# Splitting the rotated queries and keys of a decoder block over 128 rows, with the halves placed by DMA, and one step of the wide rsqrt on ScalarE

## The chip, the cores and the metric

The kernel runs on one core of a Trainium2 chip. Its engines work side by side, each on its own instruction stream: TensorE (matrix products; PE in the profile, its weight loads PEld), VectorE (DVE), ScalarE (ACT), GpSimd (POOL) and SyncE (SP). SP does nothing here but start DMAs; POOL starts those that add into their destination. All DMAs are carried out by the core's 16 DMA engines.

The metric is the time of one execution on the device in microseconds (us), lower is better. "Profiled execution" is the one execution that was recorded; its span is the time from its first to its last instruction.

## What is computed

The block has a causal pooling mixer and a causal differential attention side by side, then cross attention to a memory, then a squared-ReLU MLP, each with RMS norms. The change touches the attention's queries and keys, and the RMS norms. Cut to that (4 heads, each with 2 maps of width 64; sequence 512; model width 1024):

```python
h = rms_norm(x, g_mix)                        # x * rsqrt(mean(x*x) + 1e-6) * g
u, q, k, v, gate_logits = split(h @ w_in)
q = apply_rope(q.reshape(B, S, 4, 2, 64))     # t1*cos - t2*sin, t2*cos + t1*sin
k = apply_rope(k.reshape(B, S, 4, 2, 64))
s = einsum('bqhcd,bkhcd->bhcqk', q, k) * 64 ** -0.5
p = softmax(where(kpos <= qpos, s, -1e30))
a = p[:, :, 0] - lam * p[:, :, 1]
o = rms_norm(a @ v, g_subln) * (1 - lam_init)
```

Inputs and output are float32. The products run in a faster float32 form (`F32R` in the code), and to keep the accuracy each operand is given as a sum of two parts: a high part, the operand cast to `F32R`, and a low part, the operand minus its high part. A full product is then three matmuls: high by high, high by low, low by high.

## The kernel before

Everything is laid out with features on the 128 partitions ("rows") and the 512 positions along the free dimension. The order of TensorE's instructions is the program's own order, written out by hand: `PLAN` gives the order of the projection tiles, `k0 q0 q1 k1 q2 q3 g4 k2 g5 g6 k3 g7 u0 u1 u2 u3 g0 g1 g2 g3`, after the value projection. Each tile is eight steps of three matmuls (`tile_mm`, lines 316 to 322, `mm3`, lines 116 to 119). After each step a counter goes up by one (`tick`), and work that is due at that count is put in (`after`, `run_due`). So the scores of head h for the query block i are put in at count 36 + 6 (4 h + i) (`START`, `SPACE`, lines 593 to 595); the first, of head 0 and block 0, four steps into tile q2. The orders of the other engines and of the DMA queues are not written out: a planner arranges them when the program is built, from a model of the durations, and from then on they are fixed. Each engine then works through its list in order and waits, by semaphores, for what each instruction needs.

A projection tile of q or k (`qk_proj`, lines 443 to 462) holds one head: 128 rows, two maps of 64 (`c` is 0 or 1), with columns of the weights so arranged that the two halves of a rotation lie in neighbouring rows. VectorE multiplies the product by the table of sines into `b` and by that of cosines into `a` (lines 447 and 448). Two DMAs on POOL's queue add the neighbouring rows of `b` into `a` (line 450), and `a` is then the rotated tile. What the scores need is `s`, with 128 rows and a column block for each map c: for map 0 the high part in rows 0 to 63 and the low part in rows 64 to 127, for map 1 the other way round. One matmul over 128 rows then sums high times high and low times low (line 472), and a second one with `z`, which is the k tile with its row halves exchanged, adds high times low and low times high (line 473). The halves of `s` are written by four instructions of 64 rows each: ScalarE casts (lines 453 and 455), VectorE subtracts (lines 454 and 456), the latter reading one half of the rows and writing the other. For a k tile two DMAs on SP's queue copy `s` with its halves exchanged into `z` (lines 460 and 461), each 64 rows of 1024 values.

`tmp()` has 10 buffers of 128 x 512 in this part of the program; `a` and `b` are two of them. `s` and `z` are from a set of 6 buffers: k0, z0, q0, q1, k1 and z1 fill it, and q2, q3 and k2 can be written only after the last scores of head 0 have been read, z2, k3 and z3 only after those of head 1. The scores' products go to three PSUM banks (`sc`), and each is given back when VectorE has read it (line 476).

`split` (lines 122 to 124) makes a high and a low part of one width: a cast on ScalarE and a subtraction on VectorE. `rsqrt` (lines 242 to 251) makes rsqrt(sum * scale + eps): VectorE writes the mean plus epsilon `v` (line 244), ScalarE makes the logarithm from the same sum (line 245), an exponential (246) and a square (247), and VectorE corrects the result with `v` by one Newton step (248 and 251). It is called with a width of 512 by the first norm and by each of the four attention heads (`finish`, lines 512 to 518), with a width of 256 by the memory's norm, and with widths of 4 and 8 by the rest. `M` is 256.

Weights of the next tiles come in by loads on SP's queue (line 162), 512 KB each into three buffers `wraw`, and are split by ScalarE (line 123) and VectorE (line 124).

Of the kernel before, what the change touches and what calls it, by code (L numbers as in the profile page):

```python
# [12 lines left out]
F32R = mybir.dt.float32r  # L13
AF = mybir.ActivationFunctionType
ALU = mybir.AluOpType
# [7 lines left out]
M = 256  # L23
# [4 lines left out]
EPS = 1e-6  # L28
# [26 lines left out]
def block_kernel(ctx: ExitStack, tc: tile.TileContext, x0g, xT, memT, wv, wm, wst, wcq, wdn, wckv, wpool, vecs, csts, idn, gfin, out):  # L55
    nc = tc.nc
    ctx.enter_context(tc.manual_schedule(engines={mybir.EngineType.PE}))
    pool = ctx.enter_context(tc.tile_pool(name="sb", bufs=1))
    first, early = ExitStack(), ExitStack()
# [24 lines left out]
    def sb(tag, shape, bufs, dt=F32):  # L84
        if tag in MID_TAGS and not late:
            return mid["pool"].tile(shape, dt, tag=tag, name=nm(tag), bufs=bufs)
        if tag in STAGE_TAGS and not late:
            return stage.tile(shape, dt, tag=tag, name=nm(tag), bufs=bufs)
        p = apool if tag in EARLY_TAGS else late["pool"] if tag in LATE_TAGS else pool
        return p.tile(shape, dt, tag=tag, name=nm(tag), bufs=bufs)  # L90

    def tmp(dt=F32):
        return sb("tmp", [P, T], 3 if late else 10, dt)
# [4 lines left out]
    def pair(tag, bufs):  # L98
        return sb(tag, [P, 2, T], bufs, F32R)
# [4 lines left out]
    def acc():  # L104
        return ps("acc", 2)

    def f(ap):
        return ap.bitcast(F32)

    V = nc.vector  # L110
# [3 lines left out]
    S = nc.scalar  # L114
# [7 lines left out]
    def split(hi, lo, src, eng=V):  # L122
        S.copy(hi, src)  # L123
        eng.tensor_tensor(lo, src, f(hi), op=ALU.subtract)  # L124
# [16 lines left out]
    eps = home[:, 560:561]  # L141
# [99 lines left out]

    def rsqrt(dst, ssum, scale, v, l, by=None):

        V.tensor_scalar(v, ssum, scale, EPS, op0=ALU.mult, op1=ALU.add)
        S.activation(l, ssum, AF.Ln, bias=eps, scale=scale)
        S.activation(dst, l, AF.Exp, scale=-0.5)
        S.activation(l, dst, AF.Square)
        V.scalar_tensor_tensor(l, l, -0.5, v, op0=ALU.mult, op1=ALU.mult)
        if by is not None:
            by(dst)  # L250
        V.scalar_tensor_tensor(dst, l, 1.5, dst, op0=ALU.add, op1=ALU.mult)
# [11 lines left out]
    def rstd_full(sp, scratch, w=T):  # L263
        o = ps("tr", 2)[:, :w]
        bcast_sum(o, *sp)
        r = sb("rstd", [P, w], 1) if w == T else sb("mrstd", [P, w], 1)[:, :w]
        rsqrt(r, o, 1.0 / D, scratch, tmp()[:, :w])
        return r

    def rstd_rows(sp, n):  # L270
        hi, lo = sp
        o = ps("tr", 2)
        for i in range(n):
            c = slice(i * P, (i + 1) * P)
            nc.tensor.matmul(o[:, 2 * i:2 * i + 2], hi[:, c], ones[:, :2], start=True, stop=False)
            nc.tensor.matmul(o[:, 2 * i:2 * i + 2], lo[:, c], ones[:, :2], start=False, stop=True)
        r = sb("rrow", [P, 16], 2)[:, :2 * n]
        rsqrt(r, o[:, :2 * n], 1.0 / D, sb("rscr", [P, 8], 4)[:, :2 * n], sb("rscr", [P, 8], 4)[:, :2 * n])
        return r
# [36 lines left out]
    def tile_mm(o, w, rhs, ks=range(KC), first=True, last=True):  # L316
        ks = list(ks)
        for n, k in enumerate(ks):
            c = slice(k * P, (k + 1) * P)
            mm3(o, w[0][:, c], w[1][:, c], rhs[k][0], rhs[k][1],  # L320
                first and n == 0, last and n == len(ks) - 1)
            tick()
# [33 lines left out]
    def W(*key):  # L356
        return weights(where[key])
# [85 lines left out]
    def qk_proj(which, h):  # L443
        o = acc()
        tile_mm(o, W(which, h), xg)
        a, b = tmp(), tmp()
        V.tensor_tensor(b, o, sin_r, op=ALU.mult)
        V.tensor_tensor(a, o, cos_r, op=ALU.mult)
        for j in range(2):
            nc.gpsimd.dma_start(a[j::2, :], b[1 - j::2, :], accum_op=ALU.add)  # L450
        s = pair("s", 6)
        top, bot = slice(0, 64), slice(64, 128)
        S.copy(s[top, 0, :], a[top, :])
        V.tensor_tensor(s[bot, 0, :], a[top, :], f(s[top, 0, :]), op=ALU.subtract)
        S.copy(s[bot, 1, :], a[bot, :])
        V.tensor_tensor(s[top, 1, :], a[bot, :], f(s[bot, 1, :]), op=ALU.subtract)
        st[which, h] = s
        if which == "k":
            z = pair("s", 6)
            nc.sync.dma_start(f(z[top, :, :]), f(s[bot, :, :]))  # L460
            nc.sync.dma_start(f(z[bot, :, :]), f(s[top, :, :]))
            st["z", h] = z


# [35 lines left out]
    def attend(h):  # L500
        at = st["at", h]
        o = ps("av", 1)
        e = slice(h * P, (h + 1) * P)
        for b in range(NT):
            vh, vl = st["v"][b]
            mm3(o[:, b * P:], vh[:, e], vl[:, e], at[0][:, b, b * P:], at[1][:, b, b * P:],
                b == 0, b == NT - 1)
        sq = tmp()
        S.activation(sq, o, AF.Square)
        sp = split_sq(sq, T)  # L510

        def finish():
            s = ps("tr", 2)
            bcast_sum(s, *sp)
            y = tmp()
            rsqrt(y, s, 1.0 / P, sq, tmp(),
                  lambda r: V.scalar_tensor_tensor(r, o, st["gsub"], r, op0=ALU.mult, op1=ALU.mult))
            merge(4 + h, y)

        after(FINISH, finish)  # L520
# [68 lines left out]

    v_proj()  # L590
    tiles = {"q": lambda m: qk_proj("q", m), "k": lambda m: qk_proj("k", m), "g": gate_proj, "u": u_proj}
    for n, (kind, m) in enumerate(plan):
        if n == 2:
# [348 lines left out]
    rows = {}  # L942
# [298 lines left out]
```

## Time and profile before

| | us |
|---|---|
| three runs | 695.05, 696.56, 696.99 |
| median | 696.56 |
| profiled execution, its own time | 696.08 |
| its span | 694.3 |
| granted TensorE clock over the span | 0.996 of full speed |

The page of the profile gives each engine's busy time and then cuts the span into 40 slices of 17.4 us:

```
## 2 busy tenths in 40 slices
PE   9999999899999999999999999999999999999995
DVE  7688899886577998897488699967997779868996
ACT  7445888659655875565376967457844776367853
PEclk9999999999999999999999999999999999999999
```

Each digit is a busy share in tenths, and 9 means 90% or more. The q and k tiles, the scores and the pooling lie between 27 us and about 165 us, that is in slices 2 to 10. PE is busy nearly throughout; DVE and ACT have slices of eight or nine tenths there. Three more views are used below: the waits of an engine (who waited, for whom, how long), stretches of the span with the busy time of each engine, the granted clock and the share of the DMA engines that was busy, and the timeline, with each instruction's start and duration.

### The profile page before, as it was taken

The numbers are of one execution on the slowest core, as the hardware profiler recorded it, in microseconds if no ns is written. First come the engines' busy times: TensorE is split into PE (matmuls) and PEld (weight loads), VectorE is DVE, ScalarE is ACT, GpSimd is POOL, SyncE is SP. The second block draws the span as 40 slices with busy tenths as digits, with TensorE's granted clock in tenths as the row PEclk, the third lists the DMA queues.
The fourth block names the chain that finished last, engine by engine and source line by source line (L and its number), as shares of the span: only waits on it lengthen the run. The fifth ranks groups of instructions, "written<-read, shape, count | busy, mean of one in ns | idle before, by whom it ended". The sixth has DMA issues, their size and how long they took to land.

```text
span 694.3 us, 10735 instructions
## 1 busy us (share of the span) xinstructions
PE 682.1 (98%) x4024; PEld 603.2 (87%) x4024; DVE 562.0 (81%) x867; ACT 449.3 (65%) x726; POOL 82.3 (12%) x87
## 2 busy tenths in 40 slices
PE   9999999899999999999999999999999999999995
PEld 6888887788889979998889998899888998899884
DVE  7688899886577998897488699967997779868996
ACT  7445888659655875565376967457844776367853
POOL 0022101544210000000100011100100001100200
PEclk9999999999999999999999999999999999999999
DMA  8565325115484454430782179966688578967713
GB/s 311 173 162 157 92 82 155 67 35 209 152 244 147 156 182 121 109 106 31 209 245 92 64 202 237 257 213 183 156 246 241 153 180 211 268 182 184 167 46 121
DMA packets 34275, 113.66 MB, mean 164 GB/s; under 512 B 3984, under 2 KB 4624, under 8 KB 34224
## 3 DMA queue, kind: packets, MB, share of 16 engines
q1 hardware_dynamic: 26416, 87.42, 36.0%
q0 software_dynamic: 7664, 25.30, 20.5%
q8 instruction: 31, 0.51, 0.3%
q10 hardware_dynamic: 144, 0.26, 0.1%
q14 instruction: 20, 0.16, 0.1%
HBM read 106.68 MB, written 2.10 MB: 157 GB/s over the span
## 4 chain that ended last, share of the span: by engine, by line
PE 57%; DVE 1%; ACT 0%; DVEq 0%; issue 0%
PE sc L117 9%; PE sc L119 9%; PE sc L118 9%; PE acc L117 8%; PE acc L119 8%; PE acc L118 8%; PE tr L117 2%; PE tr L119 2%; PE tr L118 2%; PE tr L801 1%; PE tr L950 0%; PE acc L950 0%; ACT tmp L787 0%; PE av L119 0%; PE av L117 0%; PE av L118 0%
## 5 line engine op out<-in xcount | busy, mean ns | idle before, releaser
L123 ACT CAST whi<-wraw 128x1024 fp32r<-128x1024 f32 (+1 forms) x80 | 82.5, 1032 | 47.7 <-PE acc L118 16.7
L124 DVE TENSOR_TENSOR wlo<-wraw,whi 128x1024 fp32r<-128x1024 f32 (+1 forms) x80 | 97.4, 1219 | 14.5 <-ACT whi L123 14.1
L123 ACT CAST whi<-mraw 128x1024 fp32r<-128x1024 f32 x58 | 60.9, 1050 | 51.8 <-PE sc L118 14.5
L124 DVE TENSOR_TENSOR wlo<-mraw,whi 128x1024 fp32r<-128x1024 f32 x58 | 70.6, 1222 | 23.1 <-ACT whi L123 22.9
L117 PE MATMUL acc<-xg,whi 128*128 128x512 f32 x200 | 80.2, 401 | 0.0
L119 PE MATMUL acc<-xg,wlo 128*128 128x512 f32 x200 | 78.2, 391 | 0.0
L118 PE MATMUL acc<-xg,whi 128*128 128x512 f32 x200 | 78.0, 390 | 0.0
L124 DVE TENSOR_TENSOR mhl<-mraw,mhl 128x1024 fp32r<-128x1024 f32 x32 | 39.0, 1221 | 18.7 <-ACT mhl L123 18.5
L123 ACT CAST mhl<-mraw 128x1024 fp32r<-128x1024 f32 x32 | 33.7, 1052 | 30.6 <-PE sc L118 10.5
L119 PEld LDWEIGHTS acc<-xg,wlo 128*128 128x128 f32 x200 | 37.5, 188 | 8.2
L117 PEld LDWEIGHTS acc<-xg,whi 128*128 128x128 f32 x200 | 37.7, 189 | 7.2
L118 PEld LDWEIGHTS acc<-xg,whi 128*128 128x128 f32 x200 | 37.7, 189 | 7.0
L117 PE MATMUL sc<-mix,whi 128*128 128x256 f32 (+1 forms) x120 | 36.9, 307 | 0.0
L119 PE MATMUL sc<-mix,wlo 128*128 128x256 f32 (+1 forms) x120 | 36.2, 302 | 0.0
L118 PE MATMUL sc<-mix,whi 128*128 128x256 f32 (+1 forms) x120 | 36.1, 301 | 0.0
L123 ACT CAST xg<-raws 128x1024 fp32r<-128x1024 f32 x28 | 29.3, 1050 | 9.2 <-PE acc L118 4.7
L124 DVE TENSOR_TENSOR xg<-raws,xg 128x1024 fp32r<-128x1024 f32 x28 | 34.0, 1218 | 0.7 <-ACT xg L123 0.5
L184 POOL DMA_DIRECT2D mraw<-wdn x16 | 13.8, 864 | 171.1 <-DMA mraw<-wdn 79.0
L117 PE MATMUL acc<-mix,whi 128*128 128x256 f32 (+1 forms) x104 | 33.8, 325 | 0.0
L119 PE MATMUL acc<-mix,wlo 128*128 128x256 f32 (+1 forms) x104 | 33.6, 323 | 0.0
L118 PE MATMUL acc<-mix,whi 128*128 128x256 f32 (+1 forms) x104 | 33.4, 321 | 0.0
L184 POOL DMA_DIRECT2D mraw<-wst x16 | 13.8, 864 | 154.7 <-DMA mraw<-wst 95.8
(382 smaller groups left out, 2212.2 us busy)
## 6 DMA issues: line engine op xcount, KB each, us to landing
wraw<-wm SPq DMA_DIRECT2D x36, 512.0 KB, 3.3
mraw<-wst SPq DMA_DIRECT2D x24, 512.0 KB, 5.2
mraw<-wdn SPq DMA_DIRECT2D x24, 512.0 KB, 4.2
mraw<-wdn POOLq DMA_DIRECT2D x24, 512.0 KB, 7.3
wraw<-wckv SPq DMA_DIRECT2D x16, 512.0 KB, 3.7
mraw<-wst POOLq DMA_DIRECT2D x16, 512.0 KB, 7.2
wraw<-wst SPq DMA_DIRECT2D x16, 512.0 KB, 6.3
wraw<-wdn SPq DMA_DIRECT2D x16, 512.0 KB, 5.9
```

Source lines behind the costliest of these rows:

```text
L117: nc.tensor.matmul(o, lh, rh, start=start, stop=False, skip_group_check=free)
L118: nc.tensor.matmul(o, lh, rl, start=False, stop=False, skip_group_check=free)
L119: nc.tensor.matmul(o, ll, rh, start=False, stop=stop, skip_group_check=free)
L123: S.copy(hi, src)
L124: eng.tensor_tensor(lo, src, f(hi), op=ALU.subtract)
L184: nc.gpsimd.dma_start(r, part(key, then), accum_op=ALU.add)
L801: nc.tensor.transpose(tr[:, (2 * c + b) * P:(2 * c + b + 1) * P], e[:, b * M + c * P:b * M + (c + 1) * P], ident)
```

## The change

For a tile of q or k, the high and the low part are now made for all 128 rows at once by `split`, in `hi` (a further `tmp` buffer) and `lo` (the memory of `b`, whose sum has been added by then). `place` then brings their halves to `s` by four DMAs on SP's queue, each of 64 rows by 512 values, and for a k tile to `z` by four more, straight from `hi` and `lo` instead of from `s`. In `rsqrt`, where the width is 256 or more, ScalarE writes the mean plus epsilon, as an activation with a scale and a bias; the narrow ones stay on VectorE.

```diff
     def rsqrt(dst, ssum, scale, v, l, by=None):
 
-        V.tensor_scalar(v, ssum, scale, EPS, op0=ALU.mult, op1=ALU.add)
+        if v.shape[1] < M:
+            V.tensor_scalar(v, ssum, scale, EPS, op0=ALU.mult, op1=ALU.add)
+        else:
+            S.activation(v, ssum, AF.Identity, bias=eps, scale=scale)
         S.activation(l, ssum, AF.Ln, bias=eps, scale=scale)
...
         s = pair("s", 6)
         top, bot = slice(0, 64), slice(64, 128)
-        S.copy(s[top, 0, :], a[top, :])
-        V.tensor_tensor(s[bot, 0, :], a[top, :], f(s[top, 0, :]), op=ALU.subtract)
-        S.copy(s[bot, 1, :], a[bot, :])
-        V.tensor_tensor(s[top, 1, :], a[bot, :], f(s[bot, 1, :]), op=ALU.subtract)
+        hi, lo = tmp(F32R), b.bitcast(F32R)
+        split(hi, lo, a)
+
+        def place(to, first, second):
+            for c, rows in enumerate((top, bot)):
+                nc.sync.dma_start(f(to[top, c, :]), f((first, second)[c][rows, :]))
+                nc.sync.dma_start(f(to[bot, c, :]), f((second, first)[c][rows, :]))
+
+        place(s, hi, lo)
         st[which, h] = s
         if which == "k":
             z = pair("s", 6)
-            nc.sync.dma_start(f(z[top, :, :]), f(s[bot, :, :]))
-            nc.sync.dma_start(f(z[bot, :, :]), f(s[top, :, :]))
+            place(z, lo, hi)
             st["z", h] = z
```

## The prediction

> **What bounds the kernel now.** I read the page's busy times first, then what TensorE (PE) waits for, then stretches around each wait, then the timeline where the changed lines run.
>
> ```profile
> PE 682.1 (98%) x4024; PEld 603.2 (87%) x4024; DVE 562.0 (81%) x867; ACT 449.3 (65%) x726; POOL 82.3 (12%) x87
> PE sc L472 <- DVE small L476: 2.2, 1, 2.2
> PE av L118 <- DVE at L124: 0.9, 1, 0.9
> 106.81 0.50 PE L118 MATMUL av<-at,vr 128*128 128x512 f32 x1 [0.86 <-DVE at L124]
> 131.32 0.44 PE L472 MATMUL sc<-s,s 128*128 128x384 f32 x1 [2.25 <-DVE small L476]
> ```
>
> PE is busy 682.1 of 694.3 us, and its matmuls are the same in both kernels. So VectorE or ScalarE work saved is worth nothing in itself; it pays only where PE waits for it. In the attention part there are two such waits, both for VectorE (DVE): 0.86 us at 106 us and 2.25 us at 129 us. What a wait costs beyond itself shows in the stretches behind the second (columns: stretch, length, busy time of PE, PEld, DVE, ACT and POOL with instruction counts, granted clock, DMA share, GB/s):
>
> ```profile
> 130.00:132.00 2.00, 0.68 (x3) 0.65 (x4) 2.00 (x7) 1.64 (x4) 1.83 (x2) 0.98 0.00 0
> 132.00:134.00 2.00, 2.00 (x7) 1.76 (x6) 1.97 (x9) 1.10 (x4) 1.92 (x2) 0.50 0.25 66
> 134.00:136.00 2.00, 2.00 (x11) 1.87 (x10) 0.63 (x2) 0.80 (x4) 1.58 (x2) 0.66 0.52 205
> 106.00:108.00 2.00, 1.19 (x6) 1.10 (x7) 1.94 (x5) 1.95 (x4) 0.00 (x0) 1.00 0.71 262
> ```
>
> The granted clock falls to 0.50 and 0.66 of full speed for 2 us each. At half speed half the time is lost, so this loses 2 x 0.50 + 2 x 0.34 = 1.7 us more. Behind the 0.86 us wait the clock stays at 1.00. I therefore price a wait of over 2 us with a drop of 1.7 us, a shorter one without. So 0.9 + 2.25 + 1.7 = 4.8 us is all that the change could win here.
>
> [...]
>
> **What is removed.** Per tile, of eight:
>
> ```profile
> L453 ACT CAST s<-tmp x8: 602/621/622, 42.9 to 105.7; 64x512 fp32r<-64x512 f32 x8
> L456 DVE TENSOR_TENSOR s<-tmp,s x8: 687/687/687, 44.3 to 108.7; 64x512 fp32r<-64x512 f32 x8
> 102.83 0.62 ACT L123 CAST mix<-tmp 128x512 fp32r<-128x512 f32 x1 [1.17 <-DVE tmp L542]
> 104.87 0.69 DVE L124 TENSOR_TENSOR mix<-tmp,mix 128x512 fp32r<-128x512 f32 x1
> L244 DVE TENSOR_SCALAR tmp<-tr x4: 681/684/692, 92.8 to 163.8; 128x512 f32<-128x512 f32 x4
> L245 ACT ACTIVATE tmp<-tr,vx x6: 475/680/692, 30.5 to 206.8; 128x512 f32<-128x512 f32 x5, 128x256 f32<-128x256 f32 x1
> ```
>
> A cast takes 0.62 us and a subtraction 0.69 us, over 64 rows or 128. So one of each per tile goes: 8 x 0.62 = 5.0 us of ScalarE and 8 x 0.69 = 5.5 us of VectorE. The wide rsqrts move 0.68 us each for the first norm and four heads and about 0.42 us for the memory's (an estimate: the width of 256 is 0.48 us on line 245), 3.8 us in all, to ScalarE at about the same price. Their chain gets no longer: line 245 reads the same PSUM sum, and `v` is needed only three activations later. ScalarE is then about level, VectorE 9.3 us lighter.
>
> How much reaches PE is a smaller question, since VectorE catches up in between:
>
> ```profile
> 97.86 0.69 DVE L248 SCALAR_TENSOR_TENSOR tmp<-tmp,tmp 128x512 f32<-128x512 f32 x1 [0.30 <-ACT tmp L247]
> 113.50 0.69 DVE L476 CUSTOM_DVE_ANT_0 tmp<-sc,cst 128x512 f32<-128x512 f32 x1 [0.66 <-PE sc L473]
> 115.86 0.68 DVE L244 TENSOR_SCALAR tmp<-tr 128x512 f32<-128x512 f32 x1
> ```
>
> At 113.5 us VectorE waits for PE, so nothing saved before that shortens the wait at 129. Behind it only one removed instruction lies on VectorE, the 0.68 us at 115.86. At 97.86 it waits for ScalarE, which gets no lighter, and between there and the wait at 106 nothing is removed. Bounds of the gain: 0 and 4.8 us (the planner orders both engines anew and may clear both waits). I take 1.0 us: 0.68 at the second wait, whose drop stays, and about a third of the first.
>
> **What is added.** SP's queue gets four DMAs for each q tile and eight for each k tile in place of two, 48 for 8. Bytes go from 512 KB to 1024 KB per k tile, and from none to 512 KB per q tile. Above all, a q tile, which was finished by VectorE, is now finished by a DMA. That matters where PE reads soon after. The first scores (head 0, block 0) are that place:
>
> ```profile
> 44.35 0.52 SPq L460 DMA_DIRECT2D s<-s  x1
> 45.02 0.49 SPq L461 DMA_DIRECT2D s<-s  x1
> 47.48 6.89 SPq L162 DMA_DIRECT2D wraw<-wm  x2
> 49.49 0.62 ACT L453 CAST s<-tmp 64x512 fp32r<-64x512 f32 x1 [3.65 <-DMA tmp<-tmp]
> 50.14 0.69 DVE L454 TENSOR_TENSOR s<-tmp,s 64x512 fp32r<-64x512 f32 x1 [2.70 <-ACT s L453]
> 50.86 0.69 DVE L456 TENSOR_TENSOR s<-tmp,s 64x512 fp32r<-64x512 f32 x1
> 52.97 0.22 PE L472 MATMUL sc<-s,s 128*128 128x128 f32 x1
> 53.14 0.28 PE L472 MATMUL sc<-s,s 128*128 128x128 f32 x1
> ```
>
> q0's rotated tile lands at 49.4 us, its `s` is complete at 51.55, PE reads it at 52.97 (map 0) and 53.14 (map 1): 1.4 us to spare. After the change the low part is ready at 50.83 instead, the third and fourth DMAs, those of map 1, are issued behind it at half a microsecond each, the last at about 51.8. How long until it lands?
>
> ```profile
> out<-vr SPq DMA_DIRECT2D x2, 128.0 KB, 2.2
> DMA to landing us min/median/max: 2.9/4.4/5.2
> DMA to landing us min/median/max: 5.3/5.3/5.4
> 44.00:46.00 2.00, 2.00 (x11) 1.65 (x10) 1.94 (x4) 1.25 (x2) 0.27 (x1) 1.00 1.00 265
> 46.00:48.00 2.00, 2.00 (x11) 1.65 (x10) 1.45 (x2) 0.00 (x0) 1.14 (x2) 1.00 1.00 270
> 48.00:50.00 2.00, 2.00 (x10) 1.68 (x9) 0.00 (x0) 0.51 (x1) 0.55 (x1) 1.00 1.12 230
> 50.00:52.00 2.00, 2.00 (x10) 1.66 (x9) 1.79 (x3) 1.78 (x3) 0.00 (x0) 1.00 0.89 231
> 52.00:54.00 2.00, 2.00 (x13) 1.71 (x12) 2.00 (x3) 0.00 (x0) 0.59 (x2) 1.00 0.23 54
> ```
>
> The first row is the shortest 128 KB transfer of the list of DMA issues; the second is line 461 over the whole run, the third line 460 before 66 us (256 KB each). From below: 51.8 + 2.2 = 54.0, a wait of 0.9 us. With what such copies needed at that hour, 5.2 us: 57.0, a wait of 3.9. From above, by the work queued: the DMA engines are full from 44 to 52 us and busy 0.23 of the next two, and 512 KB more of k0 and 512 KB of q0 stand before the last landing; 1 MB at 265 GB/s is 4.0 us behind 52.5, then about a microsecond to land, 57.5 to 58, and k1's adding DMAs, which start then, share the engines: 59, a wait of 6. I take 3.9, from the row of the same place, and, being over 2 us, the clock drop of 1.7: 5.6 us.
>
> [...]
>
> The DMAs wait on SP for the cast and the subtraction. Behind k0's eight (from 43.5, its cast's end, to about 47.6 us) stands the weight load that now starts at 47.48: 0.1 us later. Behind q0's four stands the next one, which starts at 54 anyway (the row covers both): nothing. ScalarE, which waits for these loads to cast them, has the PE wait as cover. Without it the loads would land some 4 us late, and PE would stop at the next tile.
>
> Later tiles have more room. One place is tight:
>
> ```profile
> 59.41 0.62 ACT L453 CAST s<-tmp 64x512 fp32r<-64x512 f32 x1
> 72.30 0.22 PE L472 MATMUL sc<-s,s 128*128 128x128 f32 x1
> 118.55 0.22 PE L472 MATMUL sc<-s,s 128*128 128x128 f32 x1
> 90.02 0.47 SPq L460 DMA_DIRECT2D s<-s  x1
> 90.54 0.60 SPq L461 DMA_DIRECT2D s<-s  x1
> 94.86 0.22 PE L472 MATMUL sc<-s,s 128*128 128x128 f32 x1
> ```
>
> k1 is cast at 59.4 us and first read at 72.3, k3 at 105.7 (line 453's last) and 118.6: over 12 us for eight issues of half a microsecond and a landing of at most 5.4, so nothing. z2 gets its buffer at 90.0 us, when head 1 is done, and PE reads it at 94.9. Four DMAs in place of two carry the same bytes but end their issue 1.0 us later: the last is issued at 91.5 and, with line 461's least and median of 2.9 and 4.4 us, lands at 94.4 to 95.9. I cost this at nothing (bounds 0 and 1 us), since each copy is half as large. `hi` and the longer life of `lo` take one or two of ten buffers for up to 10 us; bounds 0 and 2 us of late VectorE work, taken at nothing.
>
> **The sum.** 696.08 (profiled execution; 1.8 of it outside the span) + 5.6 - 1.0 = 700.7. That execution lies 0.5 below the median of 696.56, inside the three runs. I forecast **700.5 us**.
>
> **The rivals.**
> 1. *Relief wins: faster.* The price is VectorE's lateness at 106 and 129 us. It decides if q0's last half lands within about 2 us of 53.1, so that no clock drop follows, and the new order clears both waits: 696.1 + 0.9 - 4.8 = 692.2; with two thirds of the 4.8, 693.8. For it: VectorE was busy 1.94 and 2.00 of the 2 us around the two waits, so that any instruction less counts there. Against: the DMA engines are full until 52 us, and VectorE waits for PE at 113.5. Chance 0.13.
> 2. *They cancel.* A wait of 3.9 with its drop against a full 4.8: 696.9; or a wait of 1.5 without a drop against a gain of 1: 696.6. Chance 0.26.
> 3. *It does less than it says*: the 128-row instructions cost as two of 64 rows. The rows of equal duration exclude this, and I give it no chance of its own.
> 4. *More than one new wait*: z2, a weight load or a missing `tmp` buffer stops PE again, over 2 us, with another drop: 700.7 + 2 + 1.7 = 704.4. For it: z2's margin is under half a microsecond. Chance 0.08.
>
> **How the numbers follow.** My forecast has chance 0.53; it covers 698.7 to 703.5. About 0.3%, 2.1 us, is what a measurement of this kernel can tell from no change. Faster 0.13, within 0.26, slower 0.53 + 0.08 = 0.61. For the range I cut rival 1 from two thirds of its relief on, about 0.1, and the outer half of rival 4, 0.04; the forecast's own upper bound lies inside: 694.0 to 704.4.
>
> **What would show it.** In the new profile a wait of PE at line 472 near 53 us, for a DMA, of 3 to 5 us, with a granted clock of about 0.5 behind it, is the forecast; one under 1 us, at full clock, makes it wrong. The waits at 106 and 129 us (later by what came before) show the gain: 0.6 to 0.9 and 1.5 to 2.2 if I am right, gone if rival 1 is. Line 123 should show eight new casts of 0.62 us, line 244 only narrow instructions, and ScalarE's total should change by less than 2 us.

## The result and the profile after

The changed kernel takes 705.6 us (median of four runs, 705.1 to 707.9) against 696.6 for the kernel before, run beside it on the same chip: a ratio of 1.0139, with a 95% interval of 1.0112 to 1.0166. It is 9 us slower. The forecast, 700.5, had the direction but 4 us of the size; the time lies above the range (694.0 to 704.4).

The profiled execution took 705.1 us, with a span of 703.0 against 694.3, so 8.7 us are to be found. The first rows are the busy times of the page, the others the view of what PE waited for (us in all, times, longest):

```profile
PE 684.9 (97%) x4024; PEld 604.9 (86%) x4024; DVE 553.0 (79%) x853; ACT 446.9 (64%) x724; POOL 82.4 (12%) x87
PE sc L479 <- DVE small L483: 4.8, 2, 3.9
PE sc L479 <- DMA s<-tmp: 1.8, 2, 1.4
PE tr L501 <- DVE tmp L490: 1.6, 2, 1.3
```

DVE's busy time fell by 9.0 us, much as worked out (9.3), and ACT's by 2.4, somewhat more than the forecast's "less than 2". The work of both engines did become less. What grew is PE's waiting. The timeline of PE shows where; the bracket gives the idle time before an instruction and what ended it:

```profile
54.76 0.30 PE L479 MATMUL sc<-s,s 128*128 128x128 f32 x1 [1.44 <-DMA s<-tmp]
55.57 0.44 PE L479 MATMUL sc<-s,s 128*128 128x128 f32 x1 [0.39 <-DMA s<-tmp]
62.74 0.38 PE L479 MATMUL sc<-s,s 128*128 128x256 f32 x1 [0.82 <-DVE small L483]
75.57 0.41 PE L501 MATMUL tr<-ident,tmp 128*128 128x128 f32 x2 [0.33 <-DVE tmp L490]
86.79 0.41 PE L501 MATMUL tr<-ident,tmp 128*128 128x128 f32 x2 [1.26 <-DVE tmp L490]
138.91 0.69 PE L479 MATMUL sc<-s,s 128*128 128x384 f32 x1 [3.93 <-DVE small L483]
```

And the stretches behind the first and the last of these (granted clock: the third number from the end):

```profile
54.00:56.00 2.00, 0.85 (x4) 0.77 (x5) 0.69 (x1) 0.29 (x1) 1.51 (x2) 0.86 1.10 307
56.00:58.00 2.00, 2.00 (x7) 1.62 (x7) 0.00 (x0) 0.00 (x0) 0.19 (x1) 0.50 0.90 307
58.00:60.00 2.00, 2.00 (x9) 1.60 (x8) 0.00 (x0) 0.00 (x0) 0.00 (x0) 0.78 1.05 254
136.00:138.00 2.00, 0.00 (x0) 0.00 (x0) 2.00 (x4) 0.41 (x1) 1.54 (x1) 0.84 0.00 0
138.00:140.00 2.00, 1.09 (x3) 1.09 (x4) 1.72 (x8) 1.11 (x5) 2.00 (x3) 0.50 0.75 231
140.00:142.00 2.00, 2.00 (x7) 1.71 (x7) 1.39 (x8) 1.83 (x6) 1.68 (x2) 0.50 0.10 35
142.00:144.00 2.00, 2.00 (x9) 1.90 (x8) 0.88 (x3) 1.05 (x2) 0.00 (x0) 0.50 0.00 0
144.00:146.00 2.00, 2.00 (x10) 1.56 (x9) 0.69 (x1) 0.64 (x2) 0.00 (x0) 0.95 0.00 0
```

Summed up, three places hold the loss:

| place | wait of PE | lost to the clock | against before |
|---|---|---|---|
| first scores, 53 to 60 us | 1.44 + 0.39 | 2 x (0.14 + 0.50 + 0.22) = 1.7 | +3.5 |
| head 0 and what follows, 62 to 87 us | 0.82 + 0.33 + 1.26 | none | +2.4 |
| the `sc` bank, near 129 us before, 135 to 146 after | 3.93 | 3.4, of which 0.8 falls into the wait | 6.6 for 3.95: +2.6 |

These three come to 8.5 us. The 0.86 us at 106 us is gone, and small waits elsewhere are 0.7 us more (0.39 at 5 us and 0.58 at 196 are new, 0.26 at 291 is gone), so that 8.3 of the 8.7 us are accounted for. The forecast has the first row only. The other two are waits for VectorE, which has become the lighter engine.

The timeline shows how VectorE can be late and idle at once. In the changed kernel, ScalarE's and VectorE's rows ahead of the first read of scores (line 483) are:

```profile
60.17 1.05 ACT L123 CAST whi<-wraw 128x1024 fp32r<-128x1024 f32 x1 [5.88 <-DMA s<-tmp]
61.25 1.23 DVE L124 TENSOR_TENSOR wlo<-wraw,whi 128x1024 fp32r<-128x1024 f32 x1 [6.24 <-ACT whi L123]
62.40 0.28 DVE L483 CUSTOM_DVE_ANT_0 tmp<-sc,cst 128x128 f32<-128x128 f32 x1
```

The scores of head 0 were there by 56 us. VectorE stood still for 6.24 us all the same, since the next instruction on its fixed list was the low part of a weight, and it reads the scores only behind that. The cast which that one needs started on ScalarE at 60.17 us. The profile puts its wait down to a DMA of a tile that it doesn't read; but PE went from tile q2 to the next at 60.16 us, and so gave a weight buffer back just then (read from the times, not shown by itself). PE was late by its own wait and clock drop. The two waits at 75 and 87 us have no such account of their own here.

### The profile page after: what moved, and what is told of

Read it like the earlier page. It is cut to its first block, busy times and chain, and to the rows that moved or that the text cites. A ratio compares the mean times of both kernels' runs of the same rounds, so it can differ in the third digit from the quotient of the medians.

```text
span 703.0 us, 10826 instructions
## 1 busy us (share of the span) xinstructions
PE 684.9 (97%) x4024; PEld 604.9 (86%) x4024; DVE 553.0 (79%) x853; ACT 446.9 (64%) x724; POOL 82.4 (12%) x87
## 4 chain that ended last, share of the span: by engine, by line
PE 82%; DVE 5%; DMA 5%; ACT 3%; issue 2%; SPq 1%; POOL 1%; DVEq 0%; ACTq 0%; POOLq 0%
PE acc L117 13%; PE acc L119 13%; PE acc L118 13%; PE sc L117 10%; PE sc L119 10%; PE sc L118 10%; PE tr L117 2%; PE tr L118 2%; PE tr L119 2%; DMA tmp<-tmp 1%; DMA s<-tmp 1%; DVE wlo L124 1%; DMA mraw<-wcq 1%; PE sc L420 1%; DMA wraw<-wm 1%
## 5 line engine op out<-in xcount | busy, mean ns | idle before, releaser
L123 ACT CAST whi<-mraw 128x1024 fp32r<-128x1024 f32 x58 | 61.0, 1051 | 51.8 <-PE sc L118 16.1
L117 PE MATMUL acc<-xg,whi 128*128 128x512 f32 x200 | 81.1, 405 | 0.0
L118 PE MATMUL acc<-xg,whi 128*128 128x512 f32 x200 | 78.8, 394 | 0.0
```

Source lines behind the costliest of these rows:

```text
L117: nc.tensor.matmul(o, lh, rh, start=start, stop=False, skip_group_check=free)
L118: nc.tensor.matmul(o, lh, rl, start=False, stop=False, skip_group_check=free)
```

## The experiments

Three theories stood at the start. A: the placement by DMAs carries nearly all of the cost. B: the Identity on ScalarE makes the longer wait on the `sc` bank. C: any edit shakes the planner's order, and with it the time. Each kernel was timed beside the kernel before, whose median in these comparisons was 695.7 to 696.5 us; ratios have their 95% interval. Waits and drops are those of one profiled execution, which can lie up to 2.6 us off the median: 704.3 us for 701.9 with the extra activation, 701.8 for 699.2 with 9 buffers, 700.5 for 698.8 with all query heads as before, 698.4 for 696.1 without the tile `v`.

### The two parts apart

**The rsqrt edit alone** (the kernel before with only the `rsqrt` hunk of the diff).

> The kernel before with the rsqrt edit alone (mean plus epsilon of the wide statistics by an Identity on ScalarE, queries and keys made as before). Theory A, that the placement of q and k by DMAs carries nearly all of the cost: 696 to 698 us, within 0.3% of before, and the wait of about 2.25 us on the sc bank near 129 us stays at 1.5 to 3 us. Theory B, that the Identity delays ScalarE's queue near 120 us and so makes the growth of the wait on the sc bank and of the clock drop behind it (3.93 us and a drop of some 2.65 us in the changed kernel against 2.25 and 1.7): 698.5 to 700 us, with a wait of 3.5 us or more near 129.

Measured: 700.1 us, 1.0051 [1.0032, 1.0070]. **The placement alone** (the diff without that hunk).

> The changed kernel with the mean plus epsilon back on VectorE: the placement alone. Theory A: 704 to 706.5 us, as the whole change (705.6), with the two waits on the first scores (1.4 and 0.4 us) and the clock drop behind them, and the long wait near 139 us. Theory B: 2.5 us less than the whole change, 702.5 to 703.5 us, the wait near 139 us at 2.5 us or less.

Measured: 704.1 us, 1.0108 [1.0089, 1.0126]. So neither theory is enough. The rsqrt edit by itself costs 3.6 us, in essence in one place: its only long wait is 5.04 us at 134 us, for 2.25 at 131 before, with the clock at half for 6.8 us for 3.4. The placement by itself costs 7.5, and on the `sc` bank it even gains: two waits of 0.75 and 1.03 us, at 134 and 141 us, and no drop. Whether the two costs, 11.1 us, add up to the whole (9.7 by the ratio) can't be told, since the intervals are wider than the difference. But their waits don't: between 53 and 95 us the placement alone has 7.1 us of them, the whole change 4.2.

**Query head 0 made as before**, in the whole change:

```diff
+        if which == "q" and h == 0:
+            S.copy(s[top, 0, :], a[top, :])
...
+            st[which, h] = s
...
+            return
         hi, lo = tmp(F32R), b.bitcast(F32R)
```

> The changed kernel, but the tile of query head 0 is made by four 64-row instructions as in the kernel before; heads 1 to 3 and all keys are placed by DMAs. Takes away what only the first scores wait for. If the first wait and its drop (1.83 + 1.56 us) and what follows them by 87 us (0.82 + 0.33 + 1.26 us) hang on q0 alone: 699.5 to 701.5 us, with no wait over 0.5 us between 50 and 90 us. If later waits are of their own making (VectorE's and ScalarE's changed order): 702 to 703 us, since only the first wait and drop go. If the order of the instructions is shaken by any edit, the wait near 129 to 139 us alone may change the result by 2 us either way.

Measured: 703.2 us, 1.0099 [1.0076, 1.0122]. The first wait and its drop are gone, but between 64 and 86 us there are 4.7 us of waits, more than the 2.4 of the changed kernel. They don't hang on query head 0. **All four query heads made as before** (the same with `which == "q"`):

> The changed kernel, but the tiles of all four query heads are made by four 64-row instructions as before; only the keys' two tiles a head are split once and placed by eight DMAs. Theory that the queries alone carry the cost, since their tiles are read soon after their products and the keys' are not: 696 to 698.5 us. Rival, that the keys' eight DMAs a head on SP's queue (a weight load behind them, two further buffers held until the last of them has landed) cost as much as the queries': 700 to 702 us.

Measured: 698.8 us, 1.0038 [1.0025, 1.0050]. PE has no wait from 20 to 120 us, so the keys' eight DMAs a head cost nothing there. What is left is 3.92 us at 133 us and its drop of 3.4. With the rsqrt edit taken out as well, that is **only the keys placed**:

> The kernel before with only the keys split once and placed by DMAs; queries and rsqrt as before. With the Identity in beside it this was 698.8 us, with no wait between 20 and 120 us and a wait of 3.92 us on the sc bank with a drop of 3.4 us behind it at 133. If that wait grew by the rsqrt edit and the placement of the keys costs nothing: 694 to 696.5 us, the wait near 129 us between 0 and 2.5 us. If the placement of the keys has a cost of its own near 129 us: 698 us or more, with a wait over 3 us.

Measured: 696.2 us, 0.9994 [0.9981, 1.0007]; the wait is 1.03 us and has no drop.

### The wait on the sc bank

**A neutral edit**, the two products swapped:

```diff
-        V.tensor_tensor(b, o, sin_r, op=ALU.mult)
         V.tensor_tensor(a, o, cos_r, op=ALU.mult)
+        V.tensor_tensor(b, o, sin_r, op=ALU.mult)
```

> The kernel before with its two products of a query or key tile swapped in the program (cosine ahead of sine): the same instructions, none added or removed, so that only the planner's order can change. Theory C, that the order of VectorE's queue near 129 us is shaken by any edit: the wait on the sc bank there changes by over 1 us or a new wait over 0.5 us appears elsewhere, and the time leaves 694.5 to 697.5 us. Theories A and B, that the cost hangs on what the edits add: 695 to 697 us, the wait near 129 us at 2 to 2.6 us.

Measured: 696.4 us, 1.0002 [0.9991, 1.0012], waits of 0.96 and 2.25 us. Theory C in its plain form falls: not any edit moves the time.

**VectorE lighter, ScalarE as before**, by leaving the tile `v` out:

```diff
-        V.tensor_scalar(v, ssum, scale, EPS, op0=ALU.mult, op1=ALU.add)
...
-        V.scalar_tensor_tensor(l, l, -0.5, v, op0=ALU.mult, op1=ALU.mult)
+        V.scalar_tensor_tensor(l, l, -0.5 * scale, ssum, op0=ALU.mult, op1=ALU.mult)
```

> The kernel before without the tile of mean plus epsilon: the Newton step reads the sum in PSUM and multiplies by scale there, so VectorE has one instruction fewer for each rsqrt, ScalarE none more, and epsilon is left out of that step. Theory B1, that the Identity's time on ScalarE makes the longer wait near 129 us: 694.5 to 696 us, the wait there at 2.25 us or less. Theory B2, that VectorE, free earlier by one instruction, is handed the split of a weight ahead of the read of the scores, so that the order makes it: 698 to 700.5 us, a wait of 3.5 us or more, with a 128x1024 subtraction ahead of the read as in the run of the rsqrt edit alone.

Measured: 696.1 us, 0.9999 [0.9984, 1.0014], the wait 1.57 us without a drop. In the profiled execution, the longest of ten, what that saves goes again in 0.34 and 1.16 us of waits and a drop of 1.7 us at 185 to 191 us. **ScalarE heavier, VectorE as before**:

```diff
         V.tensor_scalar(v, ssum, scale, EPS, op0=ALU.mult, op1=ALU.add)
+        if v.shape[1] >= M:
+            S.activation(l, ssum, AF.Identity, bias=eps, scale=scale)
```

> The kernel before with an Identity of the sum on ScalarE added ahead of each wide logarithm, into the tile that the logarithm then overwrites; VectorE keeps its mean plus epsilon. Theory B1 (ScalarE's time): 698 to 700.5 us, the wait near 129 us at 3.5 us or more. Theory B2 (VectorE's order): 695.5 to 697.5 us, the wait at 2 to 2.6 us.

Measured: 701.9 us, 1.0078 [1.0054, 1.0102], the wait 4.71 us, with 0.90, 1.16 and 0.85 us at 41, 109 and 127 us beside it. So it is the instruction added on ScalarE, not the one taken from VectorE. **All but one of them**, that of head 1 (the edit is shown against the rsqrt edit alone):

```diff
-        if v.shape[1] < M:
+        if v.shape[1] < M or st.get("head") == 1:
...
+            st["head"] = h
             rsqrt(y, s, 1.0 / P, sq, tmp(),
```

> The kernel with the rsqrt edit alone, but the rsqrt of head 1, whose Identity of 0.67 us stood at 115.8 us, keeps its mean plus epsilon on VectorE; the other four wide rsqrts keep the Identity. If the longer wait near 129 us comes from this one instruction on ScalarE, 15 us ahead of it: 695 to 697.5 us, the wait at 2.7 us or less. If it comes from the earlier ones (30.4 and 92.7 us) through the order that they give: 699 to 701 us, as the rsqrt edit alone, the wait at 3.5 us or more.

Measured: 695.6 us, 0.9999 [0.9986, 1.0011]. One instruction of 0.67 us, 15 us ahead of the wait, makes the 4 us. It can't do that by its duration. So theory B1 names the right instruction, and theory B2 the right mechanism, VectorE's order. VectorE's rows ahead of the read that PE waits for show what it does; first the kernel before, then the rsqrt edit alone, then the run without head 1's Identity:

```profile
130.26 0.67 DVE L563 TENSOR_TENSOR padu<-acc,rstd 128x512 f32<-128x512 f32 x1
130.26 0.07 DVE L562 MEMSET padu<- 128x16 f32 x1
130.84 0.41 DVE L476 CUSTOM_DVE_ANT_0 tmp<-sc,cst 128x256 f32<-128x256 f32 x1
131.19 0.08 DVE L476 DVE_READ_ACCUMULATOR2_ANT small<- 128x1 f32 x1
131.19 1.34 DVE L124 TENSOR_TENSOR wlo<-wraw,whi 128x1024 fp32r<-128x1024 f32 x1
```

```profile
130.85 0.69 DVE L566 TENSOR_TENSOR padu<-acc,rstd 128x512 f32<-128x512 f32 x1
131.47 2.31 DVE L124 TENSOR_TENSOR wlo<-wraw,whi 128x1024 fp32r<-128x1024 f32 x1
131.48 0.07 DVE L565 MEMSET padu<- 128x16 f32 x1
133.71 0.41 DVE L479 CUSTOM_DVE_ANT_0 tmp<-sc,cst 128x256 f32<-128x256 f32 x1
```

```profile
131.55 0.42 DVE L479 CUSTOM_DVE_ANT_0 tmp<-sc,cst 128x256 f32<-128x256 f32 x1
131.90 0.08 DVE L479 DVE_READ_ACCUMULATOR2_ANT small<- 128x1 f32 x1
131.90 0.69 DVE L567 TENSOR_TENSOR padu<-acc,rstd 128x512 f32<-128x512 f32 x1
```

The same instructions stand in three orders. With `padu`, a product for the pooling, ahead of the read and the low part of a weight (`wlo`) behind it, PE waits 2.25 us; with both ahead 5.04; with both behind 1.03 (the next `wlo` starts at 133.31 us), and 1.04 at the read before, at 125 us. The twenty profiles of this study fit: both ahead goes with 3.9 to 5.0 us (the changed kernel, the rsqrt edit alone, query head 0 or all queries as before beside it, the extra activation, and the last run below), `padu` alone with 2.1 to 2.3, neither with 1.0 to 1.6; in one, with later scores, there is no wait at this place. The planner chose the order when each program was built.

### The waits between 62 and 87 us

**The scores four ticks later**, in the placement alone:

```diff
-START, SPACE, SOFTMAX, ATTEND, FINISH, POOLING = 20, 6, 15, 3, 6, 23
+START, SPACE, SOFTMAX, ATTEND, FINISH, POOLING = 24, 6, 15, 3, 6, 23
```

> The placement alone, with the first scores 4 ticks (some 2.6 us) later in TensorE's order (START 24 for 20). If the waits of 2.07, 1.11 and 2.16 us at 56, 64 and 71 us all go back to the first scores' waiting for query head 0 (the later two through weight splits that the planner put ahead of the scores' reads): none over 0.5 us is left between 50 and 80 us, and 696.5 to 699.5 us. If only the first goes (2.07 us and its drop of 1.7) and the others stand by themselves: 699.5 to 702 us. If scores moved later cost as much elsewhere: 702 us or more.

Measured: 704.1 us, 1.0119 [1.0080, 1.0157]. The first wait and its drop (2.07 + 1.7 in the placement alone) are gone and the waits between 60 and 95 us halved, from 5.1 to 2.5 us. But with the later scores there are seven waits between 136 and 195 us, 6.0 in all, for 1.8 from 134 us on in the placement alone. The time is the same, so what is saved early is given back, and this doesn't settle the middle waits.

**Only tiles that are read late** (keys and query heads 2 and 3; the condition of the edit above is now `which == "q" and h < 2`, and rsqrt is as before):

> All keys and query heads 2 and 3 placed by DMAs, query heads 0 and 1 and rsqrt as in the kernel before: only tiles that are read long after they are made are placed. Theory that only a tile read soon costs: 694.5 to 697 us, no wait over 0.8 us between 60 and 100 us. Rival, that the 128-row split itself costs, since ScalarE and VectorE stand still behind it until its accumulating DMA lands (4.2 us at 67.7 and 3.2 us at 78 with heads 1 to 3 placed): waits of 0.5 to 2 us between 70 and 90 us, 698 to 700.5 us.

Measured: 695.6 us, 0.9997 [0.9982, 1.0013]. **Query head 0 alone placed** (`(which, h) != ("q", 0)`), and **query head 1 alone placed** (`(which, h) != ("q", 1)`):

> The kernel before with query head 0 alone split once and placed by four DMAs. Theory D, that the wait of the first scores for its last DMA and the order given to weight splits behind it cost by themselves: 700 to 703 us, a wait of 1.5 us or more at 54 to 57 us with a drop behind it, and waits of 1 to 3 us more until 72. Rival, that it is late only behind the eight DMAs of key head 0 on SP's queue: 696 to 698 us, the first wait under 1 us and no drop.

> The kernel before with query head 1 alone split once and placed by four DMAs. It is first read about 15 us after the first scores. Theory D, that a tile which TensorE doesn't wait for costs nothing: 695 to 697 us, no wait over 0.8 us between 50 and 95 us. Rival E, that its split stands at the head of ScalarE's queue until its accumulating DMA lands and holds back the softmax of head 0 behind it: 698 to 701 us, waits of 1 to 4 us in all between 55 and 90.

Measured: 699.2 us, 1.0041 [1.0023, 1.0060] for head 0, with a wait of 1.89 us at 56 us, a drop of 1.7 and nothing more until 110 (the wait on the `sc` bank, 2.26 us with its drop, stays as before); and 695.3 us, 0.9989 [0.9979, 0.9999] for head 1. So the first wait stands without the keys' DMAs ahead of it, but it doesn't bring the later waits by itself. **All but query head 0 placed** (`(which, h) == ("q", 0)`):

> The placement of all tiles but query head 0, with rsqrt as before. With the rsqrt edit beside it this was 703.2 us, with waits of 4.7 us in all between 64 and 86. If the parts add: some 4 us less than that, 698.5 to 700.5 us, with the same 4 to 5 us of waits between 64 and 86 (rival E). If those waits came by the rsqrt edit: 695.5 to 697.5 us, as with query heads 0 and 1 left as they were (695.6).

Measured: 699.3 us, 1.0049 [1.0034, 1.0065], with waits of 2.17, 0.41 and 1.44 us between 65 and 89. Heads 1 to 3 of the queries and the keys cost nothing in the three smaller sets above, and 3.4 us together. ScalarE's timeline ahead of the first of these waits:

```profile
60.72 0.62 ACT L123 CAST tmp<-tmp 128x512 fp32r<-128x512 f32 x1 [2.65 <-DMA tmp<-tmp]
61.25 0.40 ACT L494 ACTIVATE tmp<-tmp,small 128x128 f32<-128x128 f32 x1
62.92 1.05 ACT L123 CAST whi<-wraw 128x1024 fp32r<-128x1024 f32 x1
```

The cast of the 128-row split stood 2.65 us for its accumulating DMA, with head 0's softmax (line 494) behind it, then a weight's cast; VectorE subtracts that weight's low part ahead of the read that PE waits for:

```profile
63.04 0.35 DVE L499 SCALAR_TENSOR_TENSOR tmp<-tmp,small,tmp 128x128 f32<-128x128 f32 x1 [0.53 <-ACT tmp L498]
64.00 1.23 DVE L124 TENSOR_TENSOR wlo<-wraw,whi 128x1024 fp32r<-128x1024 f32 x1 [0.60 <-ACT whi L123]
65.14 0.42 DVE L492 CUSTOM_DVE_ANT_0 tmp<-sc,cst 128x256 f32<-128x256 f32 x1
65.62 0.45 PE L488 MATMUL sc<-s,s 128*128 128x384 f32 x1 [2.17 <-DVE small L492]
```

To test it, **the split and placement of heads 1 to 3 were emitted 8 ticks later**, with all else as in this run:

```diff
-        hi, lo = tmp(F32R), b.bitcast(F32R)
-        split(hi, lo, a)
...
+        def finish():
+            hi, lo = tmp(F32R), b.bitcast(F32R)
+            split(hi, lo, a)
...
+        if h:
+            after(8, finish)
+        else:
+            finish()
```

> The placement of all tiles but query head 0, with rsqrt as before, but split and placement of heads 1 to 3 are emitted 8 ticks (some 5.3 us) after the accumulating DMAs, behind the work that is ready by then. Theory F, that the cast stands at the head of ScalarE's queue until the accumulating DMA lands and holds back the softmax of head 0: ScalarE's waits for those DMAs fall below 1.5 us each, no wait of TensorE over 0.8 us between 60 and 95, 695.5 to 697.5 us. Theory G, that the tiles held until the placing DMAs have landed make it: tiles are held 5 us longer here, so waits as before or longer, 699 to 702 us.

Measured: 696.7 us, 1.0012 [0.9997, 1.0026]; the waits are gone but for 0.69 and 0.23 us near 85. The rows are ScalarE's waits between 50 and 100 us, first with the early split, then with the late one:

```profile
ACT tmp L123 <- DMA tmp<-tmp: 13.7, 4, 4.6
```

```profile
ACT tmp L123 <- DMA tmp<-tmp: 3.2, 3, 1.7
```

ScalarE's longest such wait is 1.7 us, a little over the 1.5 expected. That speaks for theory F: the tiles are held longer in this kernel, which theory G would have made dearer. Two limits: the planner's orders are new in this kernel too, so that the standing cast is the cause is read from rows for the wait at 65 us and argued for the others; and the length of ScalarE's waits doesn't set the price. With keys and query heads 2 and 3 placed, ScalarE waits 16.0 us in all for accumulating DMAs in the same stretch, against 17.2 with the early split (both counted with the casts of tiles made as before, which the rows above leave out), and that run loses nothing. So it must matter what stands behind the cast (argued from these two runs).

**One buffer fewer** in the kernel before asked G directly:

```diff
-        return sb("tmp", [P, T], 3 if late else 10, dt)
+        return sb("tmp", [P, T], 3 if late else 9, dt)
```

> The kernel before with 9 buffers of a 128x512 tile in its first pool for 10. Theory G, that this pool is so tight that a tile held some microseconds longer stops VectorE: 698 us or more, waits of VectorE or ScalarE on such a tile and of TensorE of over 1 us between 50 and 120 that the kernel before lacks. Theory F: 695.5 to 697.5 us, TensorE's waits as before (0.9 us near 107, 2.25 us near 129).

Measured: 699.2 us, 1.0042 [1.0025, 1.0058], but with the waits up to 135 us nearly as before and new ones of 0.98 and 1.16 us with a drop at 189 to 195. The time is theory G's, the waits aren't: nothing shows between 62 and 87 us. Nor is it shown that the pool is short, since a like pair of waits stands at this place with ten buffers too (0.34 and 1.16 us without `v`, 0.54 and 1.17 with the later scores).

### Putting it together

**The change without the parts that cost**: query heads 0 and 1 as before (`which == "q" and h < 2`), head 1's rsqrt on VectorE.

> The change without the three parts that cost: query heads 0 and 1 made as before, and the rsqrt of head 1 with its mean plus epsilon on VectorE; all keys and query heads 2 and 3 are placed by DMAs, and the other wide rsqrts have the Identity. If the parts add: 694.5 to 697 us, within 0.3% of before, waits of 2 us or less near 125 to 132 us and none over 1 us between 50 and 95. If any edit of this size reorders the queues into a long wait somewhere: 698 us or more.

Measured: 698.0 us, 1.0026 [1.0014, 1.0038]. Near 129 us it has the short order (0.74 and 1.03 us). Its loss is 0.70, 0.58 and 1.25 us between 70 and 84. The late tiles alone showed only the last of them (0.94 us at 82), the rsqrt edit without head 1 none; the whole change with query head 0 as before had all three (0.79, 0.57 and 1.92). **The change mended at its three places**, that is the late split, query head 0 as before and head 1's rsqrt on VectorE:

> The change mended at the three places: query head 0 made as before, split and placement of heads 1 to 3 emitted 8 ticks later, the rsqrt of head 1 with its mean plus epsilon on VectorE; all else as in the changed kernel. If these three are all of the cost: 695 to 697.5 us, within 0.3% of before, no wait of TensorE over 0.8 us between 40 and 100 and no drop of the clock longer than that of before. If edits together bring a wait that each alone does not: 698 us or more.

Measured: 700.8 us, 1.0071 [1.0054, 1.0088]. Between 40 and 100 us only 0.23 us of waiting is left, so the first two places are mended. The third is not: PE waits 4.46 us at 134 us, although head 1's Identity isn't there. Again the order does it:

```profile
131.63 0.68 DVE L589 TENSOR_TENSOR padu<-acc,rstd 128x512 f32<-128x512 f32 x1
132.34 1.20 DVE L124 TENSOR_TENSOR wlo<-wraw,whi 128x1024 fp32r<-128x1024 f32 x1
132.35 0.07 DVE L593 MEMSET pad<- 128x16 f32 x1
133.48 0.40 DVE L501 CUSTOM_DVE_ANT_0 tmp<-sc,cst 128x256 f32<-128x256 f32 x1
```

So that Identity is one way to the long order and not the only one. What makes the planner choose it stays open; a kernel in which the read is held ahead of the weight's split was not tried. No version beat the kernel before by over 0.3%.

## Why the prediction was partly wrong

Term by term, the sum has 5.6 at the first scores, where 3.5 was measured; -1.0 at the waits at 106 and 129 us, where it was +1.7 (2.6 more on the `sc` bank, less the 0.86 that went); and nothing for VectorE's lateness between 62 and 87 us, where it was 2.4. The last two are the steps that failed. Besides, the sum starts from an execution 0.5 us below the median, so from the median it gives 701.2 and not 700.5.

- **The bound and the prices of the instructions: right.** PE stayed the bound (busy 684.9 of 703.0 us), VectorE's saving was worth nothing in itself, and the casts and subtractions over 128 rows cost what the rows said (0.62 and 0.69 us).
- **The first scores: right mechanism, a size off.** The step "I take 3.9, from the row of the same place" took 5.2 us for the landing of copies twice as large. The last DMA of q0 was issued at 51.83 us, as worked out (51.8), and landed 3.6 us later; the row is that DMA in the changed kernel:

```profile
DMA to landing us min/median/max: 3.6/3.6/3.6
```

  The wait was 1.83 us, not 3.9 and below the sign given for it (3 to 5), the drop 1.7 as forecast: 3.5 us for 5.6. This term was too high, so it hid part of what was missing elsewhere. Query head 0 alone confirms it (1.89 + 1.7). In the bound from above, which the sum doesn't use, the "about a microsecond to land" was the author's estimate, with no row beside it.
- **"A wait of over 2 us with a drop of 1.7 us, a shorter one without": wrong as a rule.** The drop came after 1.83 us here, and not after 2.26 us with query head 1 alone. By the rule the first scores would have cost about half.
- **The gain of 1.0 us at 106 and 129 us: the wrong sign.** The step "0.68 at the second wait, whose drop stays" counted work taken off VectorE and took its order as given; a new order was allowed for in the bounds, 0 and 4.8, but only as a gain. The wait at 106 went (0.86), as it might; that on the `sc` bank cost 2.6 us more, by the order that came with the Identity on ScalarE. The sentence "Their chain gets no longer" held, for another reason than the one given: in the kernel before the logarithm started only behind VectorE's mean plus epsilon (29.78 and 30.51 us in the first norm), in the changed one behind the Identity (29.96 and 30.54). It is beside the point.
- **"Later tiles have more room" and the life of the tiles "taken at nothing": true for each, missed for all.** Keys, late queries and query head 1 cost nothing in the smaller sets. Together they cost 3.4 us, as far as the rows and the later split show through a split that stands at the head of ScalarE's queue until its accumulating DMA has landed, with a softmax behind it. The prediction named what waits behind the moved DMAs on SP, not what waits behind the cast on ScalarE.
- **The weight load "0.1 us later": wrong, and harmless there.** It started at 52.5 us, behind q0's four DMAs, for 47.5 before; the cast it feeds waited for PE, not for it (read from the times, as above).
- **The rivals.** The fourth, more than one new wait, was the nearest (704.4, chance 0.08), but with other waits than the three it names: z2 and the weight load did nothing, and no run shows a missing buffer at work. Its chance was too small, and the range ended where it began.

## What to carry to other kernels

Where engines run fixed lists, ask of every moved instruction what stands behind it on its own engine while it waits for a DMA, and put it into the program only where its data will have landed; emitting it later saved 2.6 us here, with query head 0 and rsqrt as before. Where an order is planned from modelled times, a local gain on an engine that isn't the bound is worth no more than the order that comes out, so look at the order around the longest wait, and try the parts of a change both alone and together, since neither tells the other. A lighter engine can be the late one, as VectorE was here, with 9.0 us less work.

## What the runs showed of the hardware

Between 40 and 200 us in the twenty profiles, the clock drops came in two sizes only: each lost 1.7 or 3.4 us, which is 3.4 or 6.8 us at the granted clock of 0.50. In stretches of 0.1 us, that of the kernel before runs from 131.93 to 135.34 us (0.65 from 131.9 to 132.0, 0.79 from 135.3 to 135.4, 0.50 between), which is 3.41 us; the two of the changed kernel start at 55.45 and 137.37 us and last 3.41 and 6.83 us. The wait ahead didn't decide alone: about 2.25 us had the drop in the kernel before, with the neutral edit and with 9 buffers, and none with query head 1 alone. Of twelve waits of 1.8 to 2.3 us (the 1.44 and 0.39 of the first scores taken as one) seven had a drop; the six of 3.9 us or more all had one, of 3.4 us in the changed kernel and of 1.7 with query head 0 as before, both behind 3.93 us. The least, 0.34 and 1.16 us without `v`, had one too. Three profiles have two drops (the changed kernel, query head 0 alone, 9 buffers). These start 81.9, 78.5 and 58.0 us apart, which is 24, 23 and 17 times the 3.41 us of the short drop, so in these three executions the two drops stood a whole number of such lengths apart. Why a wait of 2.25 us had a drop and one of 2.26 us had none was not shown. In these runs a wait near 2 us was thus a chance of 1.7 us more.

The copies of 64 rows by 512 values landed between 2.2 and 6.0 us after their issue. The rows are lines 461 and 462 of the changed kernel over the whole run, the first and the second of each pair of placing DMAs:

```profile
DMA to landing us min/median/max: 2.2/2.4/5.8
DMA to landing us min/median/max: 2.2/3.0/6.0
```

The long ones lie mostly between 43 and 57 us (median 3.9 us, and 2.3 from 62 us on), with the DMA engines 0.87 to 1.10 busy in the stretches of 2 us from 44 to 60 us, and that is when the first scores are read (54.76 us).

No run compares `F32R` with plain float32: that it is the faster form was not shown.
